# Mixture-of-experts stage: sums read back, added on chip and written by every block; outputs written by the second expert; 32-row blocks

## The chip, the cores and the metric

The kernel runs on one core of one Trainium2 chip. The metric is the device time of one execution in microseconds (us). Three runs of the kernel before took 1287.95, 1279.41 and 1283.04 us, a median of 1283.04 us. The profiled execution is a run of its own and took 1281.95 us.

## The reference

One decoder block on 1024 tokens of width 1024, all in fp32. The first half (normalisation, attention, a gated MLP branch, a merge) is not touched by the change, except for a few small instructions put into it. The second half is this:

```python
x1 = x + g1 * merged                                   # what the first half leaves
h  = rms_norm(x1) * (1 + scale2) + shift2              # adaLN
# group = argmax of 4, then the top 2 of that group's 8 experts; 32 experts in all
for each token and each of its two experts e, with weight w:
    a  = silu(h @ w_gate[e]) * (h @ w_up[e])           # 1024 -> 512
    y += w * (a @ w_down[e])                           # 512 -> 1024
out = rms_norm(x1 + g2 * y) * final_g
```

An expert's three matrices hold 2 MB each, so 201 MB of weights are read once.

## The kernel before

**Phase 1** ends near 700 us. It writes `h` to a DRAM tensor `h2d` and the residual `x1` to a DRAM tensor `x1d`, token by token (`r_store`). While it ends, VectorE (DVE) sorts the experts of each group by their number of tokens (`order_list`, L1604) and starts a table that gives each block its token numbers and weights (`table`, L1666).

**Phase 2** takes the 32 experts in turn. An expert's turn is called a unit here, u0 to u31. `PLAN` says how many rows of tokens each rank of a group gets: a block of 128 rows, one of 64, or two blocks. The first unit of every group is a fixed expert, and `TURNS` sets which rank follows which. In all there are 34 blocks: 17 full ones (128 rows) and 17 half ones (64 rows). u0 to u3, u5, u7, u8, u10, u16, u22 to u25 and u28 have a full block, u12 has two full ones, u17 a full and a half one, and the others have a half block. Of a unit the work is this:

- *Weights.* SyncE (SP) issues three loads of 2 MB each (`w2_load`, issue on L1343) into a ring of seven buffers. A load waits until the buffer that it overwrites has been used: by the split (DVE, L444) for a full block, by the last matmul (L1432) for a half block. `parts_of` (L1318) cuts a matrix in two halves of the rows, so that each run of memory that a partition reads is 8 KB.
- *Tokens.* GpSimd (POOL) gathers the block's rows of `h2d` by an indirect DMA, two blocks ahead (`gather`, L1364), and TensorE (PE) turns them (`x_t`, L1382 and L1392).
- *A full block* uses three passes of matmul with each operand split in a high part (ScalarE, ACT, L443) and a rest (DVE, L444; `split2`, `mm3`, L132 to L134). `jobs2` splits two jobs ahead of the matmuls. A job is two of the eight row blocks of a gate or up matrix, or one of the four of a down matrix.
- *A half block* needs no split: it multiplies in fp32, and puts the 64 rows twice into the array, side by side, each half with half of the columns (`PSH`, L1432). Its rows of activations are so kept as two half rows of 2 KB.
- *Result.* DVE scales the down product by weight and by `g2` (`y_out`, L1506 for a half block, L1510 for a full one), and POOL adds it to the rows of `x1d` in DRAM by an indirect DMA that accumulates (`y_add`, L1493).

**The end.** When the adds have landed SP loads all of `x1d` (`f_load`, L1728, eight loads of 512 KB), and behind them the last down matrix in four parts (L1348). ACT squares the rows (L1736), DVE takes the reciprocal root (L192 to L202, ten small instructions) and scales (L1746), and POOL writes the output (`to_out`, L1764). The last two units' rows are not added in DRAM: they are gathered (`l_gather`) and added on chip. `final` (L1779 to L1819) orders this end by hand. Everything else is put in order on each engine by the framework's scheduler, from the order of the jobs.

```python
return src.rearrange("(h p j) n -> p h (j n)", h=2, p=P)          # parts_of, L1320
...
if u == NE - 2:
    jobs2.hook(jd, lambda: f_load())                             # after y_out of the unit before
```

## Time and profile before

| | |
|---|---|
| median of three runs | 1283.04 us |
| profiled execution | 1281.95 us, of which the span is 1280.3 us |
| TensorE busy | 1189.3 us, 93% of the span |
| DVE, ACT, POOL busy | 820.0, 595.2, 236.3 us |
| DMA in 750 to 1212 us | 179.82 MB, 389 GB/s |
| phase 2 | from about 700 us to the end |

The span starts with the first instruction and ends with the last; all times in the rows below are counted from its start. A window row gives an engine's busy time in that stretch. "DMA share" is the mean busy share of the core's 16 DMA engines in it; near 1 they have no free time. A waits row gives an engine, the line that waited, and what it waited for.

### The profile page before, as it was taken

What the parts mean: (1) busy time and instruction counts of PE and PEld (TensorE: products, weight loads), DVE (VectorE), ACT (ScalarE), POOL (GpSimd) and SP (SyncE); (2) the same over time, 40 slices, a digit from 0 to 9 for tenths busy, and PEclk for the clock granted to TensorE, in tenths of its full rate; (3) what the DMA queues carried; (4) which work ended last, traced back from release to release, by engine and by line L of the source; (5) the groups of instructions that cost most, each with busy time, mean ns of one, the idle gap of its engine ahead of it and who ended that gap; (6) DMA issues with size and microseconds to landing.
All of it is one profiled execution on the core that took longest, in us unless ns stands there. A gap on an engine that the chain in (4) does not pass through costs nothing. (4 is left out here: it accounts for less than half of the span.)

```text
span 1280.3 us, 17327 instructions
## 1 busy us (share of the span) xinstructions
PE 1189.3 (93%) x6243; PEld 911.5 (71%) x6244; DVE 820.0 (64%) x1699; ACT 595.2 (46%) x1005; POOL 236.3 (18%) x262
## 2 busy tenths in 40 slices
PE   6999999999989999899997999999999999899881
PEld 3788887788879888688875786676665655776540
DVE  7668885568667888344598896675434612984406
ACT  4459743236535774233345585563314512773321
POOL 3510010011140001010233322212112121111114
PEclk8899999999989999899996999999999999999996
DMA  9634446566443435534766699999999999999975
GB/s 321 216 108 124 132 135 203 174 212 230 131 169 118 127 127 183 179 99 147 288 245 233 215 366 405 400 406 399 376 333 405 383 336 407 409 411 390 412 274 218
DMA packets 106885, 334.25 MB, mean 261 GB/s; under 512 B 8883, under 2 KB 52611, under 8 KB 82344
## 3 DMA queue, kind: packets, MB, share of 16 engines
q1 hardware_dynamic: 91286, 292.46, 60.3%
q0 software_dynamic: 15408, 40.59, 10.7%
q8 instruction: 50, 0.82, 0.3%
q14 instruction: 43, 0.35, 0.1%
q10 hardware_dynamic: 98, 0.03, 0.0%
HBM read 315.98 MB, written 27.54 MB: 268 GB/s over the span
## 5 line engine op out<-in xcount | busy, mean ns | idle before, releaser
L444 DVE TENSOR_TENSOR lo<-big,hi 128x1024 fp32r<-128x1024 f32 x192 | 227.7, 1223 | 44.8 <-ACT hi L443 44.3
L132 PE MATMUL ps<-big,hi 128*128 128x512 f32 x544 | 220.3, 405 | 7.8 <-ACT hi L443 7.8
L443 ACT CAST hi<-big 128x1024 fp32r<-128x1024 f32 x192 | 196.4, 1050 | 60.9 <-PE ps L134 58.3
L133 PE MATMUL ps<-big,hi 128*128 128x512 f32 x544 | 217.1, 399 | 3.3 <-DVE big L444 3.3
L134 PE MATMUL ps<-big,lo 128*128 128x512 f32 x544 | 216.3, 398 | 0.0
L443 ACT CAST hi<-st 128x512 fp32r<-128x512 f32 x192 | 116.1, 619 | 204.2 <-PE ps L133 120.1
L444 DVE TENSOR_TENSOR lo<-st,hi 128x512 fp32r<-128x512 f32 x192 | 135.5, 717 | 105.5 <-ACT hi L443 104.8
L1432 PE MATMUL ps<-big,xTh 128*64 128x256 f32 x1088 | 128.8, 383 | 0.0
L132 PEld LDWEIGHTS ps<-big,hi 128*128 128x128 f32 x544 | 105.3, 193 | 31.4 <-ACT hi L443 9.3
L133 PEld LDWEIGHTS ps<-big,hi 128*128 128x128 f32 x544 | 105.2, 193 | 29.4 <-DVE big L444 4.8
L134 PEld LDWEIGHTS ps<-big,lo 128*128 128x128 f32 x544 | 104.8, 193 | 23.1 <-DVE lo L444 1.1
L133 PE MATMUL ps<-lo,xTh 128*128 128x512 f32 x272 | 110.5, 406 | 8.4 <-DVE lo L444 8.3
L132 PE MATMUL ps<-hi,xTh 128*128 128x512 f32 x272 | 112.2, 414 | 6.2 <-ACT hi L443 6.2
L134 PE MATMUL ps<-hi,xTl 128*128 128x512 f32 x272 | 108.8, 400 | 0.3 <-DVE xTl L444 0.3
L1432 PEld LDWEIGHTS ps<-big,xTh 128*64 128x64 f32 x1088 | 74.5, 137 | 43.1 <-issue 4.6
L132 PE MATMUL ps<-hi,big 128*128 128x256 f32 (+1 forms) x256 | 88.4, 346 | 0.0
L133 PE MATMUL ps<-lo,big 128*128 128x256 f32 (+1 forms) x256 | 86.8, 339 | 0.7 <-DVE lo L444 0.7
L134 PE MATMUL ps<-hi,big 128*128 128x256 f32 (+1 forms) x256 | 86.5, 338 | 0.0
L1432 PE MATMUL ps<-big,aTh 128*64 128x512 f32 x272 | 64.7, 614 | 8.7 <-DMA big<-in_w_down_dram 8.7
L133 PEld LDWEIGHTS ps<-lo,xTh 128*128 128x128 f32 x272 | 52.0, 191 | 23.2 <-DVE lo L444 12.9
L132 PEld LDWEIGHTS ps<-hi,xTh 128*128 128x128 f32 x272 | 51.8, 191 | 23.3 <-ACT hi L443 9.2
L1469 DVE TENSOR_TENSOR sl<-sl,ps 128x512 f32<-128x512 f32 (+1 forms) x34 | 18.8, 552 | 70.0 <-PE ps L1432 48.1
(365 smaller groups left out, 1942.6 us busy)
## 6 DMA issues: line engine op xcount, KB each, us to landing
big<-in_w_gate_dram SPq DMA_DIRECT2D x32, 2048.0 KB
big<-in_w_up_dram SPq DMA_DIRECT2D x32, 2048.0 KB
big<-in_w_down_dram SPq DMA_DIRECT2D x30, 2048.0 KB
st<-in_w_in_dram SPq DMA_DIRECT2D x26, 1024.0 KB
st<-in_w_ada_dram SPq DMA_DIRECT2D x16, 1024.0 KB
st<-in_w_o_dram SPq DMA_DIRECT2D x10, 1024.0 KB
big<-in_x_dram SPq DMA_DIRECT2D x16, 512.0 KB
bias<-biasd POOLq DMA_DIRECT2D x16, 512.0 KB, 4.6
```

The lines of the kernel that those rows point to most:

```text
L132: PE.matmul(ps, lh, rh, start=start, stop=False)
L133: PE.matmul(ps, lh, rl, start=False, stop=False)
L134: PE.matmul(ps, ll, rh, start=False, stop=stop)
L443: ACT.copy(hi, src)
L444: return DVE.tensor_tensor(lo, src, f(hi), op=OP.subtract)
L1432: PE.matmul(ps[64 * c:64 * c + 64], xt[:, j, 64 * h:64 * h + 64], w[:, n * c:n * c + n], start=start, stop=stop)
L1469: DVE.tensor_tensor(s, s, PS.pop((i, "u"))[:, 0:s.shape[1]], op=OP.mult)
```

## The change

- **Blocks.** Six of the seventeen half blocks get 32 rows (u19, u21, u27, u29, u30, u31). `side` replaces `PSH`: a 32-row block stands four times in the array, each copy with a quarter of the columns. Its rows are kept as four quarter rows of 1 KB.
- **Sums.** `x1d` is now called `zd`. A block gathers its tokens' rows of `zd` (`z_get`), DVE adds `y` to them on chip, and the rows are written back by a plain indirect DMA (`z_put`). The write of a row that is a token's second visit is left out (an index out of bounds). The accumulating DMA is gone.
- **Output.** For units from u4 on each block also squares its sums (ACT, `y_sq`), takes the reciprocal root, scales by `final_g` (`y_norm`), and writes the rows of the tokens whose second expert it is to the output (`o_put`). For blocks below 128 rows the squares of a token's parts are added by a matmul with `fold`. So the load of `x1d` and all of `final` are gone.
- **Weights.** Gate and up matrices are no longer cut in halves (`h=1`): a partition reads runs of 16 KB. The down matrices keep 8 KB.
- **Tables.** One table of ranks instead of two, but new arithmetic that tells first visits from second ones (`visits`, `rows_table`), and small constants that POOL writes during phase 1.
- **Order.** POOL's order in phase 2 is now that of the program text, and the buffers are `XB, ZB, YB, HB = 2, 3, 2, 3` (gathered rows, sums, results, split operands; the splits had four). `h2d` holds its columns in another order, made by the instructions that write it.

```diff
+MANUAL = ("Pool",)
+XB, ZB, YB, HB = 2, 3, 2, 3
 PLAN = (((128, 128), (128,), (128,), (128,), (128,), (64,), (64,)),
-        ((128, 64), (128,), (128,), (64,), (64,), (64,), (64,)),
-        ((128,), (128,), (64,), (64,), (64,), (64,), (64,)),
-        ((128,), (128,), (64,), (64,), (64,), (64,), (64,)))
+        ((128, 64), (128,), (128,), (64,), (64,), (32,), (32,)),
+        ((128,), (128,), (64,), (64,), (64,), (64,), (32,)),
+        ((128,), (128,), (64,), (64,), (32,), (32,), (32,)))
...
-        return src.rearrange("(h p j) n -> p h (j n)", h=2, p=P)
+        return src.rearrange("(h p j) n -> p h (j n)", h=2 if down else 1, p=P)
...
+    def z_get(i):
+        z = wk.tile([P, D], F32, name=nm("z"), tag="z", bufs=ZB)
+        g_ = fetch(z, zd, IDX[i][0], parts(i))
+        for j, other in writes:
+            if (i < 4) == (j < 4) and group[j] != group[i] or any(i in u and j in u for u in units):
+                tc.declare_no_dep(g_.ins, other.ins, reason="a token's two experts are of one group")
...
+    def z_put(i, z):
+        p_ = put(zd, IDX[i][1], z, parts(i))
...
+    def o_put(i, y):
+        p_ = put(out, IDX[i][2], y, parts(i))
...
+    def side(c, ps, xt, i, w, inner, start, stop):
+        n, q = rows_of[c], parts(c)
+        m = w.shape[1] // q
+        for e in range(q):
+            cols_w = w[:, m * e:m * e + m]
+            if inner and q == 4:
+                cols_w = w.rearrange("k (h p j) -> k h j p", h=2, j=2)[:, e // 2, e % 2]
+            PE.matmul(ps[n * e:n * e + n, 0:m], xt[:, n * i:n * i + n], cols_w, start=start, stop=stop)
...
+    def y_out(i):
+        q = parts(i)
+        y, z = y_part(i, WGT[i]), Z.pop(i)[:, 0:D // q]
+        DVE.tensor_tensor(z, z, y, op=OP.add)
+        z_put(i, z)
+        R["yz", i] = y, z
...
+    def n_out(y, z, ss, q):
+        if q > 1:
+            ps = bank()
+            PE.matmul(ps[:, 0:1], fold[q // 4], ss, start=True, stop=True)
+            DVE.tensor_copy(ss, ps[:, 0:1])
+        rsqrt(wk, ss, 1, 1.0 / D)
+        if q == 1:
+            DVE.scalar_tensor_tensor(y, z, ss, FG, op0=OP.mult, op1=OP.mult)
+            return
+        for _, pt, sl in each_part(q):
+            DVE.scalar_tensor_tensor(y[pt], z[pt], ss[pt], FG[pt, sl], op0=OP.mult, op1=OP.mult)
...
+        if u:
+            for k, fn in enumerate((y_sq, y_norm, y_put)):
+                jobs2.hook(ju[k], lambda fn=fn, pv=pv: each(fn, pv))
+        jobs2.hook(jg[1] if u != 4 and (not u or len(cs_) + len(pv) == 2) else ju[2], lambda cs_=cs_: each(z_get, cs_))
...
+    jd = d_jobs(cs_, ring2.add(w2_load(cs_[0], w_down, True, 4)))
+    for fn in (y_out, y_sq, y_norm, y_put):
+        jobs2.hook(jd, lambda fn=fn, cs_=cs_: each(fn, cs_))
...
-    def f_load():
-        F["x"] = [bigt([4, D]), bigt([4, D])]
-        for t in range(8):
-            SP.dma_start(F["x"][t // 4][:, t % 4], x1d[t * P:t * P + P, :])
-        R["last"] = w2_load(flat[-1], w_down, True, 4)()
...
-    jobs2.hook(nj - 1, final)
-    jobs2.run()
+    with tc.manual_schedule(engines={getattr(E_, e) for e in MANUAL}) if MANUAL else ExitStack():
+        jobs2.run()
```

**DVE around a full block, before** (where the product of u5 comes out of PE; `lo` is a split's rest, `y` the scaled down product, `sl` the gate's result):

```order
L444 TENSOR_TENSOR lo_8519<-big_8248,hi_8518 128x1024
L444 TENSOR_TENSOR lo_8527<-big_8248,hi_8526 128x1024
L1510 SCALAR_TENSOR_TENSOR y_8470<-ps_8440,w_sb,g2r 128x512
L1510 SCALAR_TENSOR_TENSOR y_8470<-ps_8441,w_sb,g2r 128x512
L444 TENSOR_TENSOR lo_8536<-big_8248,hi_8535 128x1024
L444 TENSOR_TENSOR xTl_8477<-ps_8478,xTh_8476 128x512
L444 TENSOR_TENSOR xTl_8477<-ps_8485,xTh_8476 128x512
L444 TENSOR_TENSOR lo_8552<-big_8248,hi_8551 128x1024
```

**DVE at the same place in the change** (`z` are the sums, `rsq` and `ss` the reciprocal root, `fgr` is `final_g`):

```order
L1566 SCALAR_TENSOR_TENSOR y_8582<-ps_8552,w_sb,g2r 128x512
L1566 SCALAR_TENSOR_TENSOR y_8582<-ps_8553,w_sb,g2r 128x512
L444 TENSOR_TENSOR lo_8653<-big_8321,hi_8652 128x1024
L1573 TENSOR_TENSOR z_8379<-z_8379,y_8582 128x1024
...
L444 TENSOR_TENSOR lo_8678<-big_8321,hi_8677 128x1024
L202 SCALAR_TENSOR_TENSOR rsq_8618<-rsq_8618 128x1
L198 TENSOR_SCALAR rsq_8618<-rsq_8618 128x1
L202 SCALAR_TENSOR_TENSOR ss_8612<-rsq_8618 128x1
L444 TENSOR_TENSOR lo_8719<-big_8408,hi_8718 128x1024
L1602 SCALAR_TENSOR_TENSOR y_8582<-z_8379,ss_8612,fgr 128x1024
L444 TENSOR_TENSOR lo_8725<-big_8408,hi_8724 128x1024
```

The sum over `z`, the ten steps of the root and the scaling with `final_g` now stand between the splits of the next unit's weights.

**POOL while the results of u22 and u23 are added, before** (`xg` are gathered tokens, of later units):

```order
L1364 DMA xg_10968<-h2d,tok_h 128x512
L1493 DMA x1d<-y_10769,tok_sb 1024x1024
L1364 DMA xg_11136<-h2d,tok_h 128x512
L1493 DMA x1d<-y_10946,tok_sb 1024x1024
L1364 DMA xg_11270<-h2d,tok_sb 128x1024
```

**POOL while those of u22 and u23 are written, in the change** (the first `z` fetched here is that of u23):

```order
L1386 DMA z_11359<-zd,rows_i 128x1024
L1386 DMA xg_11363<-h2d,rows_i 128x1024
L1391 DMA zd<-z_11177,rows_i 1024x1024
L1391 DMA out_dram<-y_11435,rows_i 1024x1024
L1386 DMA z_11558<-zd,rows_i 128x1024
L1386 DMA xg_11562<-h2d,rows_i 128x512
L1391 DMA zd<-z_11359,rows_i 1024x1024
L1391 DMA out_dram<-y_11634,rows_i 1024x1024
```

Four indirect DMAs stand in a unit where there were two. The sums of a block are fetched one unit before they are written back.

**PE's last rows, before** (the last up matrix, the turn of its result, the last down matrix, and the sum over a token's halves):

```order
L1432 MATMUL ps_11764<-big_11625,xTh_11706 64x256 x16
L1477 MATMUL ps_11784<-ident,sl_11753 128x128 x2
L1432 MATMUL ps_11863<-big_11701,aTh_11787 64x512 x8
L1741 MATMUL ps_11891<-fs,fold 128x2
```

**PE's last rows in the change:**

```order
L1492 MATMUL ps_12731<-big_12473,xTh_12600 32x128 x16
L1598 MATMUL ps_12750<-ss_12740,fold 128x1
L1492 MATMUL ps_12731<-big_12473,xTh_12600 32x128 x16
L1540 MATMUL ps_12788<-ident,sl_12703 128x128
L1492 MATMUL ps_12792<-big_12526,aTh_12790 32x256 x16
L1598 MATMUL ps_12820<-ss_12818,fold 128x1
```

A 32-row block takes twice as many matmuls per matrix, each with half of the columns. The load of the last down matrix, which stood behind eight loads of `x1d` on SP's queue, now stands right behind that of the last up matrix.

## Rows read from the trace of the kernel before

**Rows 1.** Page, busy time by engine: microseconds, share of the span, number of instructions.

```profile
PE 1189.3 (93%) x6243; PEld 911.5 (71%) x6244; DVE 820.0 (64%) x1699; ACT 595.2 (46%) x1005; POOL 236.3 (18%) x262
```

**Rows 2.** Windows of phase 2: length, each engine's busy time, clock, DMA share, GB/s.

```profile
700.00:750.00 50.00, 47.62 (x245) 39.13 (x245) 45.34 (x75) 31.68 (x35) 14.35 (x21) 1.00 0.68 246
1100.00:1150.00 50.00, 47.44 (x216) 38.21 (x215) 45.04 (x47) 37.06 (x42) 7.49 (x6) 1.00 1.02 409
1150.00:1200.00 50.00, 46.84 (x265) 30.14 (x265) 21.60 (x23) 16.29 (x22) 9.47 (x7) 0.97 1.02 400
1225.00:1250.00 25.00, 18.28 (x132) 9.63 (x128) 2.85 (x7) 7.83 (x16) 4.56 (x5) 0.93 0.70 267
```

**Rows 3.** Waits of SP's queue, 600 to 1281 us: total, times, longest.

```profile
SPq L1343 <- DVE lo L444: 248.2, 45, 9.6
SPq L1343 <- PE ps L1432: 198.1, 41, 14.0
SPq L1728 <- DMA x1d<-y,tok_h: 24.7, 1, 24.7
```

**Rows 4.** Waits of PE, 700 to 1281 us: total, times, longest.

```profile
PE ps L1432 <- DMA big<-in_w_down_dram: 8.7, 1, 8.7
PE ps L133 <- DVE lo L444: 8.3, 12, 1.1
```

**Rows 5.** Timeline of the end: start, length, engine, instruction, count, idle before.

```profile
1235.72 3.60 PE L1432 MATMUL ps<-big,aTh 128*64 128x512 f32 x16
...
1237.72 4.01 SPq L1728 DMA_DIRECT2D big<-x1d  x8
...
1238.73 0.14 PEld L1432 LDWEIGHTS ps<-big,xTh 128*64 128x64 f32 x2 [0.29 <-DMA big<-in_w_up_dram]
1239.16 3.62 PE L1432 MATMUL ps<-big,xTh 128*64 128x256 f32 x32
...
1252.54 5.75 PE L1432 MATMUL ps<-big,aTh 128*64 128x512 f32 x16 [8.66 <-DMA big<-in_w_down_dram]
...
1271.71 0.97 POOL L1764 DMA_INDIRECT out_dram<-big,rows_o  x1 [0.30 <-POOLq L1827]
```

**Rows 6.** DMA, 750 to 1212 us: queue packets, bytes, share; issues with landing time.

```profile
q1 hardware_dynamic: 21308, 164.28, 86.3%
q0 software_dynamic: 7328, 15.15, 13.1%
...
xg<-h2d,tok_sb POOLq DMA_INDIRECT x12, 10.0
x1d<-y,tok_sb POOLq DMA_INDIRECT x12, 10.8
```

**Rows 7.** DMA, 1238 to 1250 us (loads of `x1d` and of w_down): SP's queue.

```profile
q1 hardware_dynamic: 1157, 4.24, 92.2%
```

**Rows 8.** DMA, 949 to 951 us (two adds of full blocks): POOL's queue.

```profile
q0 software_dynamic: 77, 0.31, 88.0%
```

**Rows 9.** DMA, 1262 to 1268 us (three output writes): POOL's queue.

```profile
q0 software_dynamic: 547, 2.00, 84.5%
```

**Rows 10.** DVE, groups by shape, 700 to 1281 us: busy, mean ns, idle before.

```profile
L444 DVE TENSOR_TENSOR lo<-big,hi 128x1024 fp32r<-128x1024 f32 x185 | 219.2, 1223 | 44.7 <-ACT hi L443 44.3
L1469 DVE TENSOR_TENSOR sl<-sl,ps 128x256 f32<-128x256 f32 x17 | 7.2, 421 | 48.1 <-PE ps L1432 48.1
L1746 DVE SCALAR_TENSOR_TENSOR big<-big,fs,hi 128x1024 f32<-128x1024 f32 x8 | 9.9, 1281 | 0.1
L919 DVE TENSOR_TENSOR tA<-iota_h,rc 128x256 f32<-128x256 int32 x7 | 3.0, 433 | 0.0
L202 DVE SCALAR_TENSOR_TENSOR rsq<-rsq 128x4 f32<-128x4 f32 x4 | 0.6, 162 | 0.1
```

**Rows 11.** Timeline of POOL: the adds of u22 and of u25.

```profile
1111.65 1.60 POOL L1493 DMA_INDIRECT x1d<-y,tok_sb  x1 [1.15 <-DVE y L1510]
...
1165.60 1.58 POOL L1493 DMA_INDIRECT x1d<-y,tok_sb  x1 [4.79 <-DVE y L1510]
```

More of the change, by code (lines that the diff above doesn't have):

```diff
@@ L802, in evb @@
                 DVE.scalar_tensor_tensor(gb, gb, 1.0, banks[1][s], op0=OP.add, op1=OP.mult)
-                POOL.tensor_tensor(ga, ga, gb, op=OP.add)
+                p_ = POOL.tensor_tensor(ga, ga, gb, op=OP.add)
+                with tc.issue_after(p_.ins):
+                    for step in R["later"][:8]:
+                        step()
+                    del R["later"][:8]
                 for i, m in enumerate(M[h]):
@@ L1307, in block_kernel @@
     flat = [c for u in units for c in u]
-    ends = flat[-2:]
     regs = {}
@@ new lines, in z_put @@
+    def z_put(i, z):
+        p_ = put(zd, IDX[i][1], z, parts(i))
+        for j, other in writes:
+            tc.declare_no_dep(p_.ins, other.ins, reason="a token has one first expert")
+        for other in reads:
+            tc.declare_no_dep(p_.ins, other.ins, reason="the second expert reads after the first has written")
+        writes.append((i, p_))
+    outs = []
+    def o_put(i, y):
+        p_ = put(out, IDX[i][2], y, parts(i))
+        for other in outs:
+            tc.declare_no_dep(p_.ins, other.ins, reason="a token has one second expert")
+        outs.append(p_)
@@ L1679, in table @@
                       stop=(t == 7 and k == 1))
[L1680 to L1696 removed]
+        return ps.rearrange("p (a n) -> p a n", a=2)
@@ L1761, in block_kernel @@
-    outs = []
-    def to_out(idx, xt, half=False):
-        st_ = POOL.indirect_dma_start(out=halves(out) if half else out,
-                                      out_offset=bass.IndirectOffsetOnAxis(ap=idx, axis=0), in_=xt, in_offset=None,
-                                      bounds_check=(2 * T if half else T) - 1, oob_is_err=False)
-        for other in outs:
-            tc.declare_no_dep(st_.ins, other.ins, reason="a token's row is written once")
-        outs.append(st_)
-    def l_gather():
-        F["l"] = []
-        late_i = wk.tile([P, 2], I32, name="late_i", bufs=1)
-        for j, c in enumerate(ends):
-            DVE.tensor_copy(late_i[:, j:j + 1], IDX[c])
-        for j in range(2):
-            t = wk.tile([P, D], F32, name=nm("xg"), tag="xg")
-            fetch(t, x1d, late_i[:, j:j + 1], True)
-            F["l"].append(t[:, 0:HT])
```

474 lines of the change are left out of this document (243 added, 231 removed).

## The prediction

> **What bounds the kernel now.** I first read the busy times and the windows of phase 2. PE is busy 93% of the span [rows 1] and 47 of 50 us in windows with full blocks and with half ones, while the DMA share is 1.02 there [rows 2]. So from 750 to 1200 us two things are at their limit together: the matmuls, and the weights. Then the waits. SP waits for buffers to come free, 248.2 us for splits and 198.1 us for half blocks' matmuls [rows 3], so the ring of seven is full nearly always. PE waits for almost nothing: 8.3 us for splits, and 8.7 us, once, for the last down matrix [rows 4]. The second is the end of the kernel, and the timeline shows why. The last up matrix lands at 1238.73 us, with PE waiting for it. SP has by then put eight loads of `x1d` on the queue, and the last down matrix behind them; its matmuls start at 1252.54, and the last output write is issued at 1271.71 [rows 5], 8.6 us before the end of the span. So 41.6 us go by from the last up matrix to the end, in which DMA is at 0.70 at first and PE mostly stands. **The change is worth what it takes from these 41.6 us, less what it adds to 500 us that have no free PE and no free DMA.**
>
> The sum is made against the profiled execution, 1281.95 us; it is 1.1 us below the median of the runs, and 1.65 us lie around its span.
>
> **The end.** Removed: the 24.7 us wait of SP for the adds [rows 3], `x1d`'s 4.2 MB ahead of the last down matrix, and the scaling of all rows. The wait by itself is worth nothing, since the last up matrix lands only 1 us after it. What replaces it: the last down matrix stands right behind the last up one. 2.1 MB at the stage's rate, 164.28 MB in 86.3% of 462 us = 412 GB/s [rows 6], is 5.1 us: landed at 1243.8. Then one part's matmuls, about 1.0; four pieces of `y` at no more than 0.42 each (the nearest row is 128x256 [rows 10]), 1.7; the addition 0.4; the square 0.4; fold and copy 0.5; ten steps of the root at 0.2 (162 ns and a hop [rows 10]), 2.0; four pieces of scaling, 1.7; 0.8 for hops between engines. That is 8.5: the last write is issued at 1252.3. With the same 8.6 us behind it the span ends at 1260.9, **19.4 us earlier**. Bounds: 24 if the down matrix lands with the up matrix's stragglers, 10 if it lands 9 us later.
>
> **The stage, term by term** (the end starts when the last up matrix lands, so only what moves that counts):
>
> 1. *DVE between the splits.* A full block from u5 on gains an addition and a scaling of 128x1024 (1.28 us by the nearest row) and ten steps at about 0.2, 4.5 us. In the run u22 to u25 the units follow each other at (1165.60 - 1111.65) / 3 = 18.0 us [rows 11], and DVE is busy 45.04 of 50 us [rows 2], 16.2 per unit. 16.2 + 4.5 = 20.7 is 2.7 over, 11 us in four units. Against it stand the loads already on the queue and the short units around. Between 0 and +11 I take **+4**. In stretches with half blocks (21.60 of 50 [rows 2]) it is hidden; its cover there is PE. HB, down from four to three, comes under the same bound.
> 2. *The first fetch of sums that were written.* `z_get` of u4 must wait until the sums of u0 to u3 are written. A write and a read, 10 us each to land (the nearest rows 10.8 and 10.0 [rows 6]), stand against some 12 us until u4's sums are needed. DVE would wait 8, and the splits behind it. 0 to +8, taken **+3**: PE has two jobs split ahead.
> 3. *Tables.* DVE is busy 45.34 of 50 in 700 to 750 us, while DMA is at 0.68 [rows 2]. Eight comparisons of 0.43 go [rows 10] with their matmuls; five operations of 544 elements (0.7 each) and some 40 of 0.2 come, net +8 at most. The ring is full in that time. Taken **+2**.
> 4. *16 KB runs.* SP's packets took 462 x 0.863 x 16 / 21308 = 0.299 us at 7.7 KB [rows 6], and 12 x 0.922 x 16 / 1157 = 0.153 us at 3.7 KB [rows 7]: 0.036 us per KB and 0.02 per packet. 6,700 packets fewer, by 0.02 us over 16 engines, are -9. The other end is 0, since half of the limit is PE. Taken **-3**.
> 5. *Sums by DMA.* An add's packet took 2 x 0.88 x 16 / 77 = 0.366 us [rows 8], an output's 6 x 0.845 x 16 / 547 = 0.148 us [rows 9]. 2048 adds (47 us of all engines) become 2048 reads and 2048 writes (38), with the output's writes, which stood in the end, now among them. 0 to -9, taken **-2**. POOL's two more issues per unit, some 1.5 us each, lie beside 7.5 to 9.5 busy of 50 [rows 2]. That POOL now keeps the program's order costs nothing while `z_get` stands a unit ahead.
> 6. *32-row blocks.* In the trace a half block's up matrix is 32 matmuls in 3.62 us, 0.113 each, and its down matrix 16 in 3.60, 0.225 each with twice the columns [rows 5]: the time follows the columns. A 32-row block has 160 matmuls of half the columns. At half the time each they take 9.0 us, at an unchanged 0.113 us 18.1, against 3.62 + 3.62 + 3.60 = 10.8. For six blocks that is -11 to +44. I take a little over half, and **-2**: a unit's 6.3 MB need 15.3 us at 412 GB/s, so below that PE's time is not what counts.
>
> The stage is +2, the end -19.4: 1281.95 - 17.4 = 1264.5, **forecast 1264 us**.
>
> TensorEngine Tiling (Array Packing) in the Trainium skill, Performance Considerations, counts four-fold column tiling for a stationary side of 32 and up to 4x of speed, but the same section has some 60 cycles of overhead per matmul, against many narrow ones. By its four-fold case the blocks would take term 6's lower end and the sum would be 9 us less; by its overhead there would be no gain. No row here shows a stationary side of 32; for the 64 columns the rows agree with its two-fold case.
>
> **Rivals.**
>
> *A, slower: DVE becomes the bound of every full block.* In the changed order the ten steps and the copy behind `fold` stand in between the splits, in a queue that runs in order: a step that waits for PE or ACT holds the next unit's splits, and PE has only two jobs in hand. For it: 45.04 of 50 in u22 to u25 [rows 2], and SP's largest wait is already for splits. Against it: PE waited 8.3 us for splits in all of phase 2 [rows 4]. If each of the 12 units from u5 on with full blocks stretches by 2.7 to 4.5 us, the stage takes 32 to 54 in place of the +4: 1292 to 1314, in the middle 1303. It ends above the time before as soon as the stretch is over 1.9 us per such unit. Chance 0.18.
>
> *B, no change: narrow matmuls are paid by the instruction.* At 0.113 us each a 32-row unit takes 18.1 us where the weights need 15.3. Six units by 2.8 are 17 us: 1264 + 2 + 17 = 1283. For it: their number doubles. Against it: the two rows of a half block. Chance 0.10.
>
> *C, no change: the fetched sums come late.* The two queues share the engines: where two adds ran, POOL's packets took 88.0% of them [rows 8]. A weight packet of 8 KB is 0.3 us and a gather lands after 10.0 us [rows 6]. If rows and weights take turns, the eight packets that a full block's gather has on an engine wait 8 x 0.3 = 2.4 us longer behind 16 KB. If a fetch also queues behind the two writes of the unit before and lands after 20 us, it is late: a block's sums are needed one unit (15.3 us by the weights) and one gate matrix (3.6) after they are asked for, 18.9. That is 1.1 us in each of the 16 units with short blocks, 18 us: 1282. For it: POOL's order is fixed now. Against it: the 10.0 us. Chance 0.10.
> DMA: Bandwidth & Descriptors in the Trainium skill, Queues, rings and completion order, has each engine go round its queues packet by packet, which speaks against longer weight packets beside a chain of small fetches. No row here shows 16 KB packets, so this rule carries no more than C's chance.
>
> *D, faster: the DMA terms come in full.* -9, -9 and PE's -11 from terms 4 to 6, of which the full ring lets 20 through: 1264 + 7 - 20, about 1251, and 1243 with the end's other bound. For it: share 1.02 [rows 2]. Against it: PE's 47 of 50. Chance 0.12.
>
> The forecast keeps 0.50, with 1256 to 1272 as its own range.
>
> **How the numbers follow.** About 1%, 12.8 us, is what a measurement of this kernel can tell from no change: below 1270 is faster, above 1296 slower. Faster: 0.43 of the forecast and all of D, 0.55. Slower: 0.12 of A, 0.03 of B (at its end of +44), 0.01 of C, 0.16. Same: the rest of the four, 0.07 + 0.06 + 0.07 + 0.09, 0.29. The range reaches over the forecast, B and C, and leaves out the lower half of D and the upper two thirds of A: 1245 to 1297.
>
> **What will show it.** The end: no load of the sums on SP's queue; the last down matrix landing 4 to 7 us behind the up matrix; one DVE chain of about 8 us; 20 to 25 us from the last up matrix to the end in place of 41.6. Term 1: the spacing of u22 to u25, up to 20.7 in A, near 18.5 in the forecast, and PE's wait for L444 (8.3 us now). Term 2: one DVE wait for the fetch of u4. Term 4: SP's packet time, below 0.6 us at 16 KB. Term 6: pitch of matmuls in 32-row blocks, 0.06 or 0.113. The prediction is wrong if the last up matrix lands later than about 1250 us, whatever holds it up.

## The result, and the profile after

| | before | after |
|---|---|---|
| median of the compared runs, us | 1283.82 (4 runs, 1279.41 to 1287.95) | 1343.19 (4 runs, 1341.77 to 1347.70) |
| ratio, 95% interval | | 1.0469 [1.0425, 1.0513] |
| span of the profiled execution | 1280.3 | 1342.3 |
| `y` of u29 is added (POOL starts the DMA) | 1229.11 | 1310.48 |
| from there to the end of the span | 51.2 | 31.8 |

The change is slower by 59 us, where 1264 was forecast and 1297 was the upper end. The last two lines split the span at u29's write: counted so, the end gives back 19.4 us and the stage before it takes 81 us more. The forecast counted its end from another point, the landing of the last up matrix; from there the end gives back much less (below). The busy times of the engines, as in [rows 1]:

```profile
PE 1196.8 (89%) x6710; PEld 917.7 (68%) x6710; DVE 947.1 (71%) x2099; ACT 611.9 (46%) x1046; POOL 287.2 (21%) x373
```

DVE has 127 us more to do and PE nearly the same as before, in a longer span. The windows of [rows 2], with one for the whole middle of the stage (length, PE, PEld, DVE, ACT, POOL busy, clock, DMA share, GB/s):

```profile
700.00:750.00 50.00, 45.62 (x187) 34.59 (x187) 41.38 (x87) 27.42 (x32) 14.77 (x21) 0.86 0.54 194
800.00:1200.00 400.00, 342.47 (x1997) 227.14 (x1994) 266.32 (x493) 161.21 (x223) 105.01 (x85) 0.93 0.89 354
1100.00:1150.00 50.00, 32.81 (x399) 18.84 (x395) 24.62 (x72) 8.92 (x20) 14.21 (x15) 0.84 0.94 386
1150.00:1200.00 50.00, 43.83 (x197) 33.08 (x198) 41.25 (x64) 28.52 (x35) 12.74 (x8) 0.89 0.94 377
```

The middle window of the kernel before:

```profile
800.00:1200.00 400.00, 384.50 (x2124) 260.39 (x2123) 214.43 (x237) 171.41 (x217) 74.06 (x50) 1.00 1.00 389
```

Neither of the two limits that the prediction read in [rows 2] holds now. PE stands 42 us more in these 400 us, and the granted clock of the stretch is 0.93 in place of 1.00. The two levels are 1.2 and 2.4 GHz, so 0.93 means that 0.14 of the stretch was at the lower one. By the same times of POOL as in the table (and [rows 11]), the change is behind by 14.5 us at u0, 16.9 at u3, 24.4 at u4, 42.9 at u11, 74.7 at u21, 84.1 at u25 and 81.4 at u29. The loss is spread over the stage.

The weights are not what is late: no wait of PE for a weight load is left. SP still waits for buffers as in [rows 3], 600 to 1342 us:

```profile
SPq L1366 <- DVE lo L444: 212.2, 33, 12.8
SPq L1366 <- PE ps L1492: 197.4, 38, 13.7
```

PE's waits, 700 to 1342 us, as in [rows 4] (total, times, longest):

```profile
PE ps L1598 <- ACT y L1591: 34.0, 8, 11.0
PE ps L135 <- DVE lo L444: 17.7, 10, 4.7
PE ps L134 <- ACT hi L443: 11.3, 10, 2.1
PE ps L1446 <- DMA xg<-h2d,rows_i: 9.1, 2, 6.9
PE ps L1437 <- DMA xg<-h2d,rows_i: 5.7, 3, 2.2
```

In all PE waits 86 us there; before it was 34 us from 700 us to the end. For the high parts of splits it already waited before, a row that [rows 4] doesn't show:

```profile
PE ps L132 <- ACT hi L443: 9.0, 6, 2.1
```

L1598 is the matmul with `fold`, which adds the squares of a token's parts. It stands in PE's queue among the next unit's matmuls, and waits for the square (L1591), which waits for the addition, which waits for the fetched sums. L1446 and L1437 turn the gathered tokens. One stop for `fold`, at u13 (timeline of DVE, ACT and PE: start, length, count, idle before):

```profile
1003.99 1.51 DVE L1566 SCALAR_TENSOR_TENSOR y<-ps,w_sb,g2r 64x512 f32<-64x512 f32 x2 [6.06 <-PE ps L1492]
1010.55 0.69 DVE L1573 TENSOR_TENSOR z<-z,y 128x512 f32<-128x512 f32 x1 [5.05 <-DMA z<-zd,rows_i]
1011.27 0.63 ACT L1591 ACTIVATE y<-z 128x512 f32<-128x512 f32 x1 [9.94 <-DVE z L1573]
...
1012.05 0.58 PE L1598 MATMUL ps<-ss,jp 128*128 128x1 f32 x2 [8.17 <-ACT y L1591]
```

`y` was there at 1005.5. The sums, asked for at 999.47 behind two output writes of u12, landed at 1010.55, and PE, with up matrices in the ring, stood 8.17 us for a matmul of one column. The stops at u4, u13 and u18 (6.7, 8.2 and 11.0 us) make up 25.9 of the 34.0 us. These are units whose `z_get` stands at `ju[2]` in the edit, behind the output writes of the unit before. Only between two units of one block each, and not at u4, are the sums fetched a unit ahead, as the section on the change says of all blocks. At u18, the longest stop, something else came first: DVE had to wait until an output write had left a result buffer, of which there are two (`YB`):

```profile
1113.86 1.51 DVE L1566 SCALAR_TENSOR_TENSOR y<-ps,w_sb,g2r 64x512 f32<-64x512 f32 x2 [9.21 <-DMA out_dram<-y,rows_i]
...
1119.88 0.58 PE L1598 MATMUL ps<-ss,jp 128*128 128x1 f32 x2 [10.98 <-ACT y L1591]
```

What follows a stop is seen in the clock (windows around the stop at u13):

```profile
1000.00:1003.00 3.00, 3.00 (x28) 2.05 (x28) 0.00 (x0) 0.59 (x1) 2.39 (x3) 1.00 1.02 404
1008.00:1012.00 4.00, 0.00 (x0) 0.00 (x0) 0.69 (x1) 0.72 (x2) 0.48 (x1) 0.50 0.98 412
1012.60:1016.10 3.50, 3.50 (x15) 1.66 (x14) 1.85 (x11) 0.00 (x0) 0.00 (x0) 0.50 0.69 173
```

The clock is at its upper level before the stop and falls to 1.2 GHz in it; for 3.5 us of matmuls afterwards it is still there. Fourteen matmuls of the up matrix take 3.67 us then, and a little later 24 like them 3.16 us (PE's timeline):

```profile
1012.56 3.67 PE L1492 MATMUL ps<-big,xTh 128*64 128x256 f32 x14
...
1016.80 3.16 PE L1492 MATMUL ps<-big,xTh 128*64 128x256 f32 x24
```

Behind the late requests stands POOL's queue. Its own waits, 740 to 1310 us, and its timeline from the write of u7's sums to the requests of u10:

```profile
POOL zd L1391 <- DVE z L1573: 187.9, 26, 15.8
POOL out_dram L1391 <- DVE y L1602: 73.3, 11, 13.7
```

```profile
880.41 2.05 POOL L1391 DMA_INDIRECT zd<-z,rows_i  x1 [7.47 <-DVE ol L1764]
892.47 0.98 POOL L1391 DMA_INDIRECT out_dram<-y,rows_i  x1 [10.01 <-DVE y L1602]
893.75 1.81 POOL L1386 DMA_INDIRECT z<-zd,rows_i  x1 [0.30 <-issue]
895.87 1.04 POOL L1386 DMA_INDIRECT xg<-h2d,rows_i  x1 [0.30 <-issue]
897.21 2.02 POOL L1391 DMA_INDIRECT zd<-z,rows_i  x1 [0.30 <-DVE rsq L192]
903.92 0.99 POOL L1391 DMA_INDIRECT out_dram<-y,rows_i  x1 [4.69 <-DVE y L1602]
905.22 1.64 POOL L1386 DMA_INDIRECT z<-zd,rows_i  x1 [0.30 <-issue]
907.16 1.02 POOL L1386 DMA_INDIRECT xg<-h2d,rows_i  x1 [0.31 <-issue]
```

Each request for sums and tokens goes out right behind the output write of an earlier block, and that write waits for DVE's last scaling (L1602). The tokens asked for at 907.16, those of u12's first block, came 20.1 us later, and PE stood for them:

```profile
927.23 1.73 PE L1446 MATMUL ps<-ident,xg 128*128 128x128 f32 x7 [6.94 <-DMA xg<-h2d,rows_i]
...
930.46 0.63 PE L134 MATMUL ps<-hi,aTh 128*128 128x512 f32 x1
930.89 0.63 PE L135 MATMUL ps<-lo,aTh 128*128 128x512 f32 x1
...
932.65 0.40 PE L134 MATMUL ps<-hi,aTh 128*128 128x512 f32 x1
932.89 0.40 PE L135 MATMUL ps<-lo,aTh 128*128 128x512 f32 x1
```

Here too the matmuls behind the stop start 0.43 us apart, and 0.24 us apart two microseconds later.

The end, as in [rows 5] (the write of u29's sums, the second half of the last up matrix, the last down matrix, the last output write):

```profile
1310.48 1.00 POOL L1391 DMA_INDIRECT zd<-z,rows_i  x1 [0.31 <-issue]
...
1321.14 1.81 PE L1492 MATMUL ps<-big,xTh 128*32 128x128 f32 x32
...
1324.42 3.64 PE L1492 MATMUL ps<-big,aTh 128*32 128x256 f32 x32 [0.41 <-ACT aTh L1542]
...
1336.62 0.97 POOL L1391 DMA_INDIRECT out_dram<-y,rows_i  x1 [4.81 <-DVEq L1883]
```

From these up matmuls to the end of the span are 21.2 us, but that is not the stretch of the forecast, which ran from the landing of the last up matrix: 41.6 us before, 20 to 25 forecast. PE no longer waits for that landing, nor for the last down matrix. SP's queue, 1310 to 1325 us:

```profile
q1 hardware_dynamic: 240, 0.84, 14.7%
```

Of the last down matrix (2.1 MB) no more than 0.84 MB were still to come at 1310; from 1306 on the same view has 2.12 MB. So by estimate the last up matrix had landed near 1306, 36 us before the end. By the forecast's own mark the end gives back some 6 us, and the last up matrix is some 67 us late. What the end waits for is no longer a load. The writes of u29, u30 and u31 are issued at 1310.48, 1320.51 and 1330.84, 10.0 and 10.3 us apart, DMA's share from 1320.5 to 1330.8 is 0.02, and PE stands 2.1, 2.6 and 3.1 us for the last three sums over parts.

### The profile page after: what moved, and what is told of

Its sections match the earlier page's. It is cut to its first block, busy times and chain, and to the rows that moved or that the text cites. A ratio compares the mean times of both kernels' runs of the same rounds, so it can differ in the third digit from the quotient of the medians.

```text
span 1342.3 us, 18936 instructions
## 1 busy us (share of the span) xinstructions
PE 1196.8 (89%) x6710; PEld 917.7 (68%) x6710; DVE 947.1 (71%) x2099; ACT 611.9 (46%) x1046; POOL 287.2 (21%) x373
## 4 chain that ended last, share of the span: by engine, by line
PE 53%; DVE 16%; DMA 11%; issue 10%; ACT 3%; POOL 3%; POOLq 0%; ACTq 0%; DVEq 0%; SPq 0%
PE ps L135 13%; PE ps L136 13%; PE ps L134 13%; PE ps L1492 7%; DMA xg<-h2d,rows_i 5%; DVE lo L444 4%; DMA st<-in_w_in_dram 2%; DMA z<-zd,rows_i 2%; DVE y L1566 2%; ACT hi L443 1%; DMA st<-in_w_ada_dram 1%; PE ps L663 1%; DVE acc L255 1%; DVE z L1573 1%; DVE rsq L198 1%
## 5 line engine op out<-in xcount | busy, mean ns | idle before, releaser
L444 DVE TENSOR_TENSOR lo<-big,hi 128x1024 fp32r<-128x1024 f32 x192 | 231.0, 1220 | 57.4 <-ACT hi L443 55.8
L444 DVE TENSOR_TENSOR lo<-st,hi 128x512 fp32r<-128x512 f32 x192 | 135.2, 715 | 104.4 <-ACT hi L443 103.7
L135 PE MATMUL ps<-lo,xTh 128*128 128x512 f32 x272 | 116.3, 428 | 17.4 <-DVE lo L444 17.4
L134 PE MATMUL ps<-hi,xTh 128*128 128x512 f32 x272 | 118.1, 436 | 10.0 <-ACT hi L443 10.0
L1492 PE MATMUL ps<-big,xTh 128*32 128x128 f32 (+1 forms) x1472 | 123.6, 349 | 0.3 <-issue 0.3
L136 PE MATMUL ps<-hi,xTl 128*128 128x512 f32 x272 | 114.0, 419 | 0.1
L1566 DVE SCALAR_TENSOR_TENSOR y<-ps,w_sb,g2r 128x512 f32<-128x512 f32 (+2 forms) x80 | 52.5, 667 | 67.1 <-PE ps L1492 44.0
L1492 PEld LDWEIGHTS ps<-big,xTh 128*32 128x32 f32 (+1 forms) x1472 | 74.1, 129 | 37.3 <-issue 14.6
L135 PEld LDWEIGHTS ps<-lo,xTh 128*128 128x128 f32 x272 | 55.5, 204 | 34.5 <-DVE lo L444 21.0
L1391 POOL DMA_INDIRECT out_dram<-y,rows_i x30 | 36.2, 1208 | 200.1 <-DVE y L1602 73.3
L134 PEld LDWEIGHTS ps<-hi,xTh 128*128 128x128 f32 x272 | 55.0, 203 | 29.5 <-ACT hi L443 13.2
```

Source lines behind the costliest of these rows:

```text
L134: PE.matmul(ps, lh, rh, start=start, stop=False)
L135: PE.matmul(ps, lh, rl, start=False, stop=False)
L136: PE.matmul(ps, ll, rh, start=False, stop=stop)
L444: return DVE.tensor_tensor(lo, src, f(hi), op=OP.subtract)
L1391: return POOL.indirect_dma_start(out=in_parts(dst, q), out_offset=bass.IndirectOffsetOnAxis(ap=idx, axis=0), in_=t[:, 0:D // q], in_offset ...
L1492: PE.matmul(ps[n * e:n * e + n, 0:m], xt[:, n * i:n * i + n], cols_w, start=start, stop=stop)
```

## The experiments

Each median stands beside runs of the kernel before on the same chip. "Against the change" is the difference to its 1343.19.

**Earlier requests for the sums.** `z_early`: 1330.39 us, ratio 1.0357 [1.0328, 1.0386], 13 us less than the change. In its trace the stops for `fold` at u13 and u18 shrink to 3.4 and 8.0 us; that at u4 stays, with 6.9.

```diff
-jobs2.hook(jg[1] if u != 4 and (not u or len(cs_) + len(pv) == 2) else ju[2], lambda cs_=cs_: each(z_get, cs_))
+jobs2.hook(jg[1] if u != 4 else ju[0], lambda cs_=cs_: each(z_get, cs_))
```

> Edit: every block's fetch of its sums is issued at the start of its unit, also behind units of two blocks (u4 keeps its place but for two jobs). Theory L (sums and tokens that arrive late hold PE, and PE's clock falls behind each stop): the two waits of 8.2 and 11.0 us at the sum over a token's parts go, with some 5 to 10 us of slow clock behind them, 1343 to about 1316 (1310 to 1325). Rival N (the 32-row blocks are the loss) and rival F (the matmul that sums the parts stands too early in PE's order, whatever the fetch): within 5 us of 1343.

The result lies between the two expectations.

**And the tokens too, tried twice.** `z_and_tokens_early`: 1368.05, ratio 1.0654 [1.0622, 1.0686]. `tokens_early2`: 1326.78, ratio 1.0337 [1.0312, 1.0362].

```diff
# z_early, and in z_and_tokens_early
-jobs2.hook(jd, ahead(i, rows=not u))
-if u:
-    jobs2.hook(jg[1], ahead(i, x=False))
+jobs2.hook(jd, ahead(i))
# in tokens_early2, ahead() also gathers right behind x_t(flat[i + 1])
-if rows and i + 2 < len(flat):
-    gather(flat[i + 2])
+if i + 3 < len(flat):
+    gather(flat[i + 3])
# and once, ahead of the stage
+gather(flat[2])
```

> Edit: the same, and each block's tokens are asked for right behind the turn of the tokens before, ahead of the output's write in POOL's order. Theory L: the five waits of PE for tokens, 14.8 us, go too, with their slow clock: another 15 to 25 us, 1343 to about 1296 (1285 to 1310). Rivals N and F: 1330 or more.

> Edit: as in the run with early sums, and a block's tokens are asked for as soon as the turn of the tokens two blocks before has freed their buffer, so two entries of POOL's order earlier than in the change. Theory L: PE's waits for tokens, 14.8 us, go with their slow clock, 1330 of the early sums to about 1308 (1298 to 1318). Rival D: 1325 or more.

The first had the opposite effect of what I meant: the place `jd` lies behind the write of the sums of the unit before, so the request went out later. PE's waits in it, 740 to 1310 us:

```profile
PE ps L1446 <- DMA xg<-h2d,rows_i: 28.4, 6, 9.9
PE ps L1437 <- DMA xg<-h2d,rows_i: 23.4, 8, 5.7
```

The miss shows the sensitivity: with no work added, a request one place later in POOL's order cost 38 us against `z_early`. Two places earlier gained 4 us, which the intervals don't tell from nothing: `tokens_early2` missed its 1308 and came out where the rival had it (1325 or more).

**32-row blocks undone.** `rows64`: 1351.21, ratio 1.0537 [1.0507, 1.0566].

```diff
-        ((128, 64), (128,), (128,), (64,), (64,), (32,), (32,)),
-        ((128,), (128,), (64,), (64,), (64,), (64,), (32,)),
-        ((128,), (128,), (64,), (64,), (32,), (32,), (32,)))
+        ((128, 64), (128,), (128,), (64,), (64,), (64,), (64,)),
+        ((128,), (128,), (64,), (64,), (64,), (64,), (64,)),
+        ((128,), (128,), (64,), (64,), (64,), (64,), (64,)))
```

> Edit: the six 32-row blocks get 64 rows again, the rest of the change stays. Rival N: 20 us or more faster, 1323 or less. Theory L: within 10 us of 1343, since a 64-row unit waits in the same way; the unit's matmuls alone differ by some 2 us each.

8 us slower than the change: the small blocks gain, and are no part of the loss. In its trace u29's write comes at 1310.00 us, as in the change, and the end is 3.9 us longer; no gain of the small blocks shows in the stage.

**No sum over a token's parts.** `no_part_sum` leaves out the matmul with `fold` and its copy: 1340.11, ratio 1.0435 [1.0393, 1.0477].

```diff
-        if q > 1:
-            ps = bank()
-            PE.matmul(ps[:, 0:1], fold[q // 4], ss, start=True, stop=True)
-            DVE.tensor_copy(ss, ps[:, 0:1])
```

> Leaves out the sum of squares over a token's parts (the matmul and its copy); each part is normalised by its own sum. Rival F: PE's 34 us at that matmul go and nothing takes their place, 1309 or less. Theory L: PE goes on, but DVE still stands at the addition until the sums arrive, so half of it comes back as late splits and late products: 1318 to 1333.

3 us less, within the spread of the runs, and neither expectation (1309 or less, 1318 to 1333) came true. The matmul that stops is not the cause of the stop. PE's longest wait, 740 to 1310 us, is now for the gate's result:

```profile
PE ps L1540 <- DVE sl L1530: 30.9, 6, 10.3
```

L1530 stands behind the addition of the sums in DVE's queue, and waits with it.

**POOL's order left to the scheduler.** `pool_free`: 1328.62, ratio 1.0355 [1.0318, 1.0392].

```diff
-    with tc.manual_schedule(engines={getattr(E_, e) for e in MANUAL}) if MANUAL else ExitStack():
+    with ExitStack():
```

> Edit: POOL's order in phase 2 is left to the scheduler again, as before the change; nothing else. Theory L (POOL's fixed order lets fetches of sums and tokens stand behind an output's write that waits for the root; they land late and hold PE, whose clock then falls): the waits for sums and tokens shrink to half or less, 1343 to 1305 (1290 to 1320). Rival D (the work that DVE got between the splits): 1333 or more.

The fixed order costs 15 us, about what the earlier requests gain within it; this lies between the two expectations. From 740 to 1310 us PE's waits for tokens fall to 3.1 us, from 14.8, but those for `fold` are 32.6, from 28.3.

**Parts of the normalisation left out.** `no_norm` leaves out square, root and scaling (the output is the unscaled `y`): 1293.41, ratio 1.0091 [1.0065, 1.0116]. `no_root` leaves out the ten steps of the root: 1325.89, ratio 1.0341 [1.0303, 1.0380]. `no_out_write` writes the output of the last unit only: 1317.56, ratio 1.0272 [1.0211, 1.0333]. `no_fetch` takes `y + y` for the sums and fetches none: 1314.20, ratio 1.0239 [1.0201, 1.0278].

```diff
# no_norm
-            for k, fn in enumerate((y_sq, y_norm, y_put)):
+            for k, fn in ((2, y_put),):
...
-    for fn in (y_out, y_sq, y_norm, y_put):
+    for fn in (y_out, y_put):
# no_root
-        rsqrt(wk, ss, 1, 1.0 / D)
# no_out_write, in y_put
-        if i >= 4:
+        if i in units[-1]:
# no_fetch
-        g_ = fetch(z, zd, IDX[i][0], parts(i))
...
-        DVE.tensor_tensor(z, z, y, op=OP.add)
+        DVE.tensor_tensor(z, y, y, op=OP.add)
```

> Leaves out the squares, the root and the scaling of every block; the unscaled results are written to the output's rows. Rival D: DVE's waits and PE's waits for splits (31 us) fall to those of before (17), 1343 to 1310 or less, and waits for sums and tokens stay. Theory L: the output's write no longer waits for the root, so POOL moves on: waits for tokens go, those for the sums at three places stay: 1343 to about 1310 (1295 to 1325), so the waits tell and not the time.

> Leaves out the ten small steps of the root in phase 2 (2 us of DVE per block); squares, matmul over the parts, scaling and writes stay. Rival D: 2 us in each of 30 blocks beside splits, half of it on the path: 1343 to 1315 or less. Theory L: the write is ready 2 to 5 us earlier, which helps a little: 1325 to 1340.

> Leaves out the output's write of every block but the last; squares, root and scaling stay. Leaving out the whole normalisation gave 50 us. Theory L (POOL's queue is held by the output's write, which waits for the root, and the result buffer by its landing): most of that comes, 1343 to about 1305 (1295 to 1318). Rival D (the small steps on DVE and PE's matmul over the parts): 1330 or more.

> Leaves out the fetch of the sums; the addition adds the result to itself, so DVE has the same work, and nothing waits for sums that were written. Theory L: PE's 26 us at three sums over parts go, with the slow clock behind them, and POOL has one transfer less per unit: 1343 to about 1300 (1290 to 1315). Rival D: 1328 or more.

Against the change: -50, -17, -26 and -29 us. No one of them is the whole. Counted to u29's write in the traces (1269.65, 1291.99, 1275.55 and 1275.79 us), the stage is still 41, 63, 46 and 47 us behind that of the kernel before, where the change is 81 behind. So some 10 of `no_norm`'s 50 us are gained behind u29's write, where its end takes 21.2 us in place of 31.8; in `no_out_write` and `no_fetch` the end takes 8 us longer, and the stage gains 35. `no_norm`'s time is where the rival had it (1310 or less), but the waits that were to decide between the two decide for neither: PE's waits for splits are 24.7 us, where the rival had 17, and those for tokens 10.4, where the theory had none.

`no_norm` gains far more than `no_root`, though it keeps the output writes. POOL's timeline of `no_norm` at the place shown above shows one reason:

```profile
868.03 2.05 POOL L1391 DMA_INDIRECT zd<-z,rows_i  x1 [14.38 <-DVE ol L1764]
870.39 0.99 POOL L1391 DMA_INDIRECT out_dram<-y,rows_i  x1 [0.31 <-issue]
871.68 1.05 POOL L1386 DMA_INDIRECT z<-zd,rows_i  x1 [0.30 <-issue]
873.04 1.64 POOL L1386 DMA_INDIRECT xg<-h2d,rows_i  x1 [0.30 <-issue]
```

The same two requests follow the write of the sums after 3.7 and 5.0 us, in the change after 13.3 and 15.5: the output write no longer waits for DVE. `no_out_write` takes two waits away at once, that of the requests behind the write and that of DVE for a result buffer, and so can't tell them apart.

**Later scaling, and more buffers.** On top of `tokens_early2`: `norm_late` does the scaling and the output write one job later, 1326.32, ratio 1.0344 [1.0307, 1.0381]; `more_results` has four result buffers and two of split operands, 1336.17, ratio 1.0394 [1.0353, 1.0435]; `repaired` has those and does seven of the ten root steps on POOL, 1392.66, ratio 1.0853 [1.0818, 1.0888].

```diff
# norm_late
+            for k, fn in ((0, y_sq), (3, y_norm), (3, y_put)):
# more_results, repaired
+XB, ZB, YB, HB = 2, 3, 4, 2
# repaired, in the root's three rounds
+            POOL.tensor_scalar(a, y, h, y, op0=OP.mult, op1=OP.mult)
+            POOL.tensor_scalar(y if i < 2 else v, a, 1.5, y, op0=OP.add, op1=OP.mult)
```

> Edit: sums and tokens asked for early (the run of 1327 us), and root, scaling and write moved from the second and third job of the up matrix to its last, so that PE reaches the sum over the parts later. If PE's stops at that matmul (32.8 us there) are paid by its place: 1327 to about 1305 (1295 to 1315). If they are paid by the late result only, 1322 or more.

> Edit: the run with early sums and tokens (1327 us) with four result buffers in place of two, paid with two split buffers in place of three. Theory L (a result buffer is held until the output's write has landed, 25.4 us of DVE's waits there): those waits go, PE's stops at the sum over parts with them, 1327 to about 1308 (1298 to 1318). Rival H (the splits need their third buffer): 1327 or more.

> Edit: the same, and seven of the root's ten steps on POOL in place of DVE. Theory L with the root's 17 us: 1300 (1290 to 1312). If DVE's queue has no part in it: as the run before it. Against the kernel before, 1283, no theory expects a gain.

`norm_late` is the same as `tokens_early2`, as its second expectation had it. `more_results` is slower, as its rival had it (1327 or more), and `repaired` missed both of its expectations by far. In `norm_late` the wait only moves (740 to 1310 us): that for `fold` falls from 32.8 us to 19.2, and that for the rests of splits (L444) rises from 16.7 to 28.6.

DVE's wait for a result buffer, 9.2 us in the change, is 25.4 us in `tokens_early2`, in three stops; in `more_results` it is gone. PE's waits for `fold` fall by 14.8 us there, but its waits for splits, with two buffers in place of three, rise by 12.1. What more result buffers alone are worth is so left open.

In `repaired` DVE stands 69.6 us for the root's result from POOL, each time ahead of a scaling (L1618, L1621) and so ahead of the next splits.

**Small edits, in the kernel before.** `before_3bufs` gives the splits three buffers: 1285.51, ratio 1.0020 [1.0004, 1.0036]. `before_permuted` stores `h` in the order of columns that the change needs (its products are of other columns): 1287.81, ratio 1.0040 [1.0019, 1.0060].

```diff
# before_3bufs
-    h2p = p2.enter_context(tc.tile_pool(name="p2hl", bufs=4, reuse_waits="tile"))
+    h2p = p2.enter_context(tc.tile_pool(name="p2hl", bufs=3, reuse_waits="tile"))
# before_permuted, in r_store; POOL's product ahead of it writes in the same order
-        DVE.scalar_tensor_tensor(h2, h2, ss, RW[1], op0=OP.mult, op1=OP.add)
+        hv = h2.rearrange("t (j p) -> t j p", j=8)
+        DVE.scalar_tensor_tensor(hv, hv, ss, RW[1].rearrange("t (p j) -> t j p", j=8), op0=OP.mult, op1=OP.add)
```

> The kernel before with three buffers in place of four for split operands, nothing else. Theory L: no change, 1278 to 1290. Rival H (the missing split buffer costs the late splits): 1295 or more.

> The kernel before with the change's order of columns in the stored tokens, written by strided operations of DVE and POOL at the end of phase 1; nothing reads them in that order, so the products are of other columns. Theory T (these strided writes delay the first tokens by 7.7 us): 1283 to about 1290 (1287 to 1293). If the first tokens' delay is made up in phase 2: within 2 us of 1283.

**The length of the runs.** `runs8k` is the change with 8 KB runs for gate and up, and the stored columns in the order that goes with them: 1315.90, ratio 1.0239 [1.0202, 1.0275], 27 us less. `before_16k` is the kernel before with 16 KB runs (and the permuted store): 1287.42, ratio 1.0027 [1.0005, 1.0048]. `runs8k_early` is `runs8k` with the requests of `tokens_early2`: 1310.65, ratio 1.0198 [1.0170, 1.0226].

```diff
# runs8k (in before_16k the other way round); the edit of the stored columns is left out here
-        return src.rearrange("(h p j) n -> p h (j n)", h=2 if down else 1, p=P)
+        return src.rearrange("(h p j) n -> p h (j n)", h=2, p=P)
```

> The change with gate and up matrices in runs of 8 KB again, and the tokens' columns ordered to match. Theory of the sum: 0 to 9 us slower than 1343, 1343 to 1352. Rival R (long packets make small fetches land late): 5 us or more faster, below 1338.

> The kernel before with 16 KB runs for gate and up, and the stores in the permuted order that they need (before_permuted, that order alone: 1287.8). Its tokens are gathered two blocks ahead and its adds are waited for by nobody. Theory (16 KB runs cost only by making dependent fetches late): 1284 to 1293, within 5 us of before_permuted. Rival (term 4 of the prediction: fewer packets move the weights faster): 1276 to 1282. Rival (the long packets cost by themselves, in the weights' own rate): 1300 or more, toward the 27 us that they cost in the change. A value of 1294 to 1299 would say that the gathers of tokens two blocks ahead are made late too.

> 8 KB runs for gate and up (as runs8k, 1315.9), and with them the fetches asked for earlier (as tokens_early2, 1326.8: the sums one gate matrix earlier, the tokens three blocks ahead). Theory (sums and tokens that land late behind long packets are one cause, and the two edits cure the same lateness in part): the 27 us of runs8k and the 16 us of tokens_early2 do not add up in full; about 1304 us, 1296 to 1314; PE's wait for the fold below 25 us. Rival (they are separate causes): 1343 - 27 - 16 = 1300 or less, which can't be told from the first unless it comes below 1296. Rival (the early requests cost what they gain once packets are short, since a fetch then lands in time anyway): 1313 to 1320, no change against runs8k. No theory expects less than 1283: the normalisation in the stage stays.

The gather that took 20.1 us in the change takes 11.8 here (timeline of `runs8k`, POOL and PE):

```profile
898.76 1.02 POOL L1387 DMA_INDIRECT xg<-h2d,rows_i  x1 [0.31 <-issue]
...
910.59 0.96 PE L1447 MATMUL ps<-ident,xg 128*128 128x128 f32 x7 [0.77 <-DMA xg<-h2d,rows_i]
```

And SP's queue, 800 to 1300 us, first in the change, then in `runs8k` (packets, MB, share):

```profile
q1 hardware_dynamic: 13981, 157.05, 78.7%
```

```profile
q1 hardware_dynamic: 21174, 160.88, 79.5%
```

500 x 0.787 x 16 / 13981 is 0.450 us per packet of 11.2 KB, and 500 x 0.795 x 16 / 21174 is 0.300 us per packet of 7.6 KB: per KB 0.040 and 0.039. The long runs gain nothing in the weights' own rate. In `before_16k` they lose nothing either (the median is 0.4 us below `before_permuted`), with the ring as full as before:

```profile
800.00:1200.00 400.00, 386.65 (x2141) 259.74 (x2142) 215.06 (x237) 172.63 (x218) 73.14 (x50) 0.99 0.99 390
```

The profiled execution of `before_16k` was a late one (1293.0 us), and its trace shows where: u0's add comes 10.3 us later than before, u29's 10.7 later, so the stage in between takes the same time. Yet a full block's gather landed later there too, after 11.4 us in the median (750 to 1212 us), 9.6 in `before_permuted`. So the 27 us are not the price of the packets but of what waits behind them: they appear only where PE depends on a chain of small fetches. `runs8k_early` gains 5 us more, hardly clear of noise, and not 16, which agrees with long packets and late requests being largely one lateness. It is the fastest of the whole forms of the change, and still 2% behind the kernel before.

## Why the prediction was wrong

**What held.** The loads of the sums and the wait for the adds are gone, and the last down matrix follows the up matrix directly. The DMA price in term 5 held: from 740 us to the end POOL's queue took 65.0 us of all engines (10.8% of 602.3) in place of 74.0 (13.7% of 540.3), the 9 us that were reckoned. They bought nothing, since DMA was no longer at its limit. Term 2's mechanism and bound: u4's sums were asked for at 812.23, when u3's write (issued 800.85) had landed, and the delay grows by 7.5 us from u3 to u4, near the upper end of 8. Term 6's sign: -2 forecast, and `rows64` says -8. The sign of being wrong that the prediction named came true: the load of the last up matrix was issued at 1299.09 us, so it landed well behind 1250.

**The step that failed** is the one that all terms of the stage share, written in term 2 as "PE has two jobs split ahead" and in term 5 as "That POOL now keeps the program's order costs nothing while `z_get` stands a unit ahead". I priced each new operation by its busy time, and its wait by whether a free buffer stood in front of PE. But the new operations put waits *into* the queues that run in order: `fold` in PE's, the addition in DVE's ahead of `sl` and the splits, the output write in POOL's ahead of the next requests. And `z_get` doesn't stand a unit ahead at u4, u13 and u18, the three longest stops for `fold`. Four edits that take no arithmetic from PE, DVE or ACT show what the waits are worth: `z_and_tokens_early` against `z_early` (+38 us), `no_out_write` (-26), `no_fetch` (-29) and `runs8k` (-27). Write, request, landing, addition, square, root, scaling, write looks like a ring that closes on itself: what is late in one unit makes a later request late. This is my reading of the orders; no run shows the lateness passed on from unit to unit. The pieces, taken out one at a time, give 3 (`no_part_sum`) to 50 us (`no_norm`) where terms 1, 2 and 5 together had +5; they overlap, so I can't split the 81 us among them. The prediction also read PE's waits for splits as 8.3 us; with those for the high parts, 9.0, it was 17.3, and 29.0 in the change.

**The end** was to go by loads, with 22.2 us from the landing of the last up matrix. By estimate it took 36 us, against 41.6 before: PE was behind the loads, and the last two units went through the chain of small steps at 10 us each. That 19.4 us come out when the span is cut at u29's write is chance.

**Term 1** (+4) had the price of the root right (2.0 us; 1304.18 to 1306.23 in the trace). In the run u22 to u25 the spacing is

```profile
1190.06 1.73 POOL L1391 DMA_INDIRECT zd<-z,rows_i  x1 [6.04 <-DVE z L1573]
...
1249.68 1.00 POOL L1391 DMA_INDIRECT zd<-z,rows_i  x1 [5.62 <-DVE z L1573]
```

(1249.68 - 1190.06) / 3 = 19.9 us against 18.0 in [rows 11]: 1.9 us per unit, where I had 18.5 and rival A 20.7. It is just the point from which A said that it would decide. A is right as to DVE's queue: `no_root` gives 17 us. It is not the whole: with no normalisation at all u29 comes 41 us later than before (1269.65).

**Term 3** (+2) measured +14.5 at u0. `before_permuted` gives 5 us to the strided stores of `h`, for which I had no term. For the rest I have only the trace: the first tokens are turned at 694.66 us, 7.7 later than before, and the clock is 0.86 in 700 to 750 us. No run separates it, and part of it is spread: in `no_part_sum`, `no_norm`, `no_out_write` and `no_root`, which differ from the change only from u4 on, u0's write is 8.3 to 12.2 us later than before.

**Term 4** (-3) had the wrong sign. Two points of mean packet time were drawn as a line with 0.02 us per packet; between 7.6 and 11.2 KB the packet's time is proportional to its bytes within 2%. Measured: 0 for the rate, and +27 us by lateness. This is rival C's mechanism, which I had put at 18 us and 0.10, against it the 10.0 us of [rows 6], a landing with one gather under way and 8 KB packets. With several indirect transfers behind each other and 16 KB packets one gather of tokens took the 20 us that C assumed for the sums. The sums of u13 took 11.1 us and were late since they were asked for late. DMA: Bandwidth & Descriptors in the Trainium skill, Queues, rings and completion order, lets each engine change queues only at the end of a packet; the gathers' 11.4 us in `before_16k`, 9.6 in `before_permuted`, agree with that.

**Term 6**: 80 gate and up matmuls (the up matrix of u29, then part of u30's gate) took 2.52 us, 0.032 each, half the columns of a half block's 0.113 in under a third of the time:

```profile
1300.85 2.52 PE L1492 MATMUL ps<-big,xTh 128*32 128x128 f32 x80
```

Half the columns and twice the copies would be a quarter of 0.113, 0.028. At this pitch, and with a down matrix of 32 matmuls in 2.00 us, a 32-row unit takes 6.0 us of PE, less than the 9.0 that the term had as its lower end. TensorEngine Tiling (Array Packing) in the Trainium skill, Performance Considerations, has four-fold column tiling for a stationary side of 32, and the row agrees with it; the overhead per matmul that the same section states did not take the gain away. Rival B falls, and of D only this term gained time.

**What stays open.** How much of the 81 us is the lower clock behind the stops, and how much the stops: PE is idle 42 us more than before in the 400 us of the middle window, and a clock of 0.93 over 342 busy us is at most some 24 more by estimate (part of the low clock lies in the stops themselves, where it costs nothing), but no run held the clock and let the stops be. Nor is it known why `no_norm`, with no root and no `fold`, is still 41 us behind at u29.

## What to carry to other kernels

In a stage that was full on two resources, a new operation can cost far more by what its wait holds up than by its busy time: for each one write down which queue it stands in, what is behind it there, and when its input was asked for. A write that waits for arithmetic doesn't belong ahead of the next unit's requests in the same in-order queue. Long packets on the bulk queue cost nothing here while nobody waited for a small fetch, and 27 us where a chain of them fed the next step. A gain at the end is counted from a point that the change doesn't move itself, and the same one before and after.

## What the runs showed of the hardware

- Runs of 16 KB for gate and up have no better rate than runs of 8 KB: 0.040 and 0.039 us per KB of one engine's time, at means of 11.2 and 7.6 KB per packet.
- A gather of 128 rows took 20.1 us to land beside 16 KB packets and 11.8 beside 8 KB ones, in the same place of the program (one pair). In the kernel before, the medians are 11.4 us (`before_16k`) and 9.6 (`before_permuted`).
- After a stop of PE of 8.17 us the clock was at 1.2 GHz for the 3.5 us of matmuls that followed. One wait so costs twice: PE's waits from 700 us to the end rose from 34 to 86 us, and matmuls behind the stops ran at the lower clock on top.
- Seven small steps per block moved from DVE to POOL cost 56 us (`repaired` against `more_results`). They take 0.27 to 0.35 us each there, 0.14 to 0.27 on DVE, and DVE then stood 69.6 us for their result.
